# Strassen's products for most input projections of the second layer of a four-layer model on one core

## The chip, the core and the metric

The kernel runs on one core of a Trainium2 chip. The time is what the device takes for one execution, in microseconds. The core's engines are TensorE (PE, the matmuls; PEld is its loading of weights), VectorE (DVE), ScalarE (ACT), GpSimd (POOL) and SyncE (SP, which here only issues transfers). Each runs its own instructions in the order in which they stand in its queue, and waits on semaphores for the others.

## What is computed

A sequence of 1024 tokens with 16 learned ones ahead, 1040 in all, 1024 features each, passes through four residual layers: sliding-window attention, a gated linear recurrence (mLSTM), another one (HGRN2), and attention again. All of it is float32. The change is in the second layer:

```python
def mlstm_branch(u, w_in, conv_w, conv_b, gate_bias, h_gain, w_out, valid):
    q, k, v, ig, fg, og, z = _split(u @ w_in, B_SIZES)   # 1024, 1024, 2048, 8, 8, 2048, 2048
    qk = jax.nn.silu(causal_conv(jnp.concatenate([q, k], axis=-1), conv_w, conv_b))
    ...
    h = mlstm_chunkwise(qh, kh, vh, log_i, log_f)        # 8 heads, 128 keys, 256 values, blocks of 128
    h = jax.nn.sigmoid(og).reshape(...) * h
    h = rmsnorm(h, h_gain.reshape(B_HEADS, B_DV)).reshape(bsz, lp, B_W)
    return (h * jax.nn.silu(z)).astype(u.dtype) @ w_out

# for each layer i
u = rmsnorm(h, norm_gain[i])
h = h + branch(u, ...)
```

## The kernel before

Features lie on the partitions. `x` is the residual, one tile of 128 x 8 x 1040; `uh` and `ul` hold the normed tokens. A float32 factor is split into a high part of a shorter format (fp32r, which PE takes at full pace) and a low part, the rest: `split` is a cast on ACT (L212) and a subtraction on DVE (L213). A product of two float32 matrices is then three matmuls, high by high, high by low and low by high (`uh,wh`, `ul,wh`, `uh,wl` in the profile).

Tokens go in three chunks of 400, 384 and 256. `proj` (L253 for its matmuls) makes one tile of 128 output features: for each chunk 8 contraction tiles of 128 by 3 products, 24 matmuls that add up in one PSUM bank, and then `evac`, which takes the bank's content on: for a query or key the causal convolution (L1031 to 1045), for `og` a sigmoid times h (L1204), for `z` a silu times h (L546, L547). `sigmoid_from` (L525 to 529) makes the sigmoid. `weights` loads a tile of weights in two halves (L229, on SP) into one of two raw buffers and splits them into one of three buffers each for `wh` and `wl`. Values are made by `proj_vt`, and the output projection by `proj_out`: L397 for its matmuls, L400 for the addition to `x`.

The second layer has eight heads. `mixer(h)` is the recurrence of one head, with small matmuls and a chain through ACT and DVE (L1086 to L1179); `weave` mixes its steps with the projections of q for head h+1, k for h+2 and v for h+1. Then follow `og` (two tiles), `z` (two tiles), with three `stat` steps between (the norm of h, L1223), and then the output projection of this head, `oc[h]`. So q, k, v are made in the mixer's stage, and a head's h is done with after its own output projection; those of heads 6 and 7 are handed to the next layer's start.

The order on PE is the order in which the steps stand in one list, written out by hand; `later` puts a step some time behind the start of a list. Weights are asked for ahead, when the steps between add up to 12 us (`LOOKAHEAD`). Instructions of the other engines, SP's transfers among them, are put in order by a scheduler when the program is built. PSUM has 8 banks.

## Time and profile before

| | us |
|---|---|
| median of 3 runs | 2565.74 (2564.76 to 2566.45) |
| the profiled execution | 2567.49 |
| its span | 2565.7, so 1.8 lie around it |
| PE busy | 2523.8 |
| DVE busy | 2025.6 |
| ACT busy | 1750.1 |
| POOL busy | 245.8 |
| moved by DMA | 140.24 MB, 55 GB/s in the mean |

The granted clock of PE is 0.999 of full speed. A row of a view gives start and length of an instruction, its engine, its line in the kernel, the operation, and what it writes and reads by the program's names; "idle before" is the time its engine stood still just ahead of it, with what ended that. A row of a table by stage has, for a stretch from one time to another, the busy time of each engine with its number of instructions in brackets, the granted clock, the busy share of the DMA engines and the GB/s. Matmuls are pipelined, so a matmul's cost is read from the step between the starts of one and the next, not from its length.

### The profile page before, as it was taken

How to read it: one execution, taken by the hardware profiler on the slowest of the kernel's cores; microseconds unless marked ns; L12 is line 12 of the kernel's file. 1: busy time of each engine (PE TensorE's matmuls, PEld its weight loads, DVE VectorE, ACT ScalarE, POOL GpSimd, SP SyncE). 2: the span in 40 equal slices, each digit the busy share in tenths (PEclk: the TensorE clock that was granted, in tenths of full speed). 3: DMA queues.
4: the chain of work that ended last, by engine and by line, in shares of the span. 5: the costliest groups of instructions: out<-in, count | busy, mean ns of one | idle time of the engine just before them, and what ended most of it. 6: DMA issues, size and time to landing. Idle time of an engine off the chain costs nothing. (4 is left out here: it accounts for less than half of the span.)

```text
span 2565.7 us, 54823 instructions
## 1 busy us (share of the span) xinstructions
PE 2523.8 (98%) x20278; PEld 2471.9 (96%) x20278; DVE 2025.6 (79%) x5593; ACT 1750.1 (68%) x4719; POOL 245.8 (10%) x569
## 2 busy tenths in 40 slices
PE   9999999999999999999999999999999999999999
PEld 8899999999999999999999999999999999999999
DVE  7897898786767676767677788988878988987986
ACT  8766767576565656565675758877676857867772
POOL 0321221000000000000000001100010100321220
PEclk9999999999999999999999999999999999999999
DMA  5223112022232212121221111111111013212112
GB/s 159 62 58 96 58 55 69 27 56 51 50 51 50 46 50 51 46 51 49 48 52 55 54 44 34 35 35 35 43 34 42 28 52 94 65 49 77 56 38 83
DMA packets 103342, 140.24 MB, mean 55 GB/s; under 512 B 15369, under 2 KB 58514, under 8 KB 103074
## 3 DMA queue, kind: packets, MB, share of 16 engines
q1 hardware_dynamic: 102786, 136.20, 19.2%
q8 instruction: 160, 2.62, 0.4%
q14 instruction: 108, 0.88, 0.1%
q10 hardware_dynamic: 288, 0.52, 0.1%
HBM read 121.83 MB, written 4.27 MB: 49 GB/s over the span
## 5 line engine op out<-in xcount | busy, mean ns | idle before, releaser
L253 PE MATMUL pj<-uh,wh 128*128 128x384 f32 (+2 forms) x2688 | 901.7, 335 | 2.1 <-ACT uh L212 1.2
L253 PE MATMUL pj<-ul,wh 128*128 128x384 f32 (+2 forms) x2688 | 864.3, 322 | 1.0 <-DVE ul L473 0.5
L253 PE MATMUL pj<-uh,wl 128*128 128x384 f32 (+2 forms) x2688 | 863.7, 321 | 0.0
L253 PEld LDWEIGHTS pj<-uh,wh 128*128 128x128 f32 x2688 | 507.2, 189 | 10.6 <-issue 2.6
L253 PEld LDWEIGHTS pj<-ul,wh 128*128 128x128 f32 x2688 | 507.8, 189 | 5.6 <-DVE ul L213 1.4
L253 PEld LDWEIGHTS pj<-uh,wl 128*128 128x128 f32 x2688 | 506.8, 189 | 0.0
L213 DVE TENSOR_TENSOR wl<-wr,wh 128x512 fp32r<-128x512 f32 (+1 forms) x336 | 231.6, 701 | 70.7 <-ACT wh L212 68.2
L212 ACT CAST wh<-wr 128x512 fp32r<-128x512 f32 (+1 forms) x336 | 201.9, 613 | 92.0 <-PE pj L397 37.8
L397 PE MATMUL pj<-yh,wh 128*128 128x384 f32 (+2 forms) x768 | 252.7, 329 | 8.0 <-DVE x L400 5.3
L400 DVE TENSOR_TENSOR x<-x,pj 128x384 f32<-128x384 f32 (+2 forms) x480 | 234.2, 507 | 32.5 <-PE pj L397 31.3
L397 PE MATMUL pj<-yl,wh 128*128 128x384 f32 (+2 forms) x768 | 246.1, 320 | 1.3 <-DVE yl L213 1.3
L397 PE MATMUL pj<-yh,wl 128*128 128x384 f32 (+2 forms) x768 | 245.9, 320 | 0.0
L809 ACT ACTIVATE Sm<-Sm,s 128x257 f32<-128x257 f32 (+2 forms) x272 | 131.1, 483 | 91.5 <-DVE s L806 86.1
L812 POOL TENSOR_TENSOR Sm<-Sm,s 128x512 f32<-128x512 f32 (+2 forms) x136 | 137.0, 1007 | 401.4 <-DVE s L811 391.8
L529 ACT ACTIVATE t<-t 128x256 f32<-128x256 f32 (+2 forms) x240 | 118.2, 492 | 66.5 <-DVE t L528 65.7
L212 ACT CAST yh<-r 128x384 fp32r<-128x384 f32 (+2 forms) x120 | 57.0, 478 | 149.0 <-PE pj L397 131.3
L397 PEld LDWEIGHTS pj<-yh,wh 128*128 128x128 f32 x768 | 144.6, 188 | 11.7 <-DVE x L400 7.3
L397 PEld LDWEIGHTS pj<-yl,wh 128*128 128x128 f32 x768 | 144.7, 188 | 2.5 <-DVE yl L213 2.2
L358 PE MATMUL pj<-wh,uh 128*128 128x256 f32 (+1 forms) x504 | 145.8, 289 | 0.0
L397 PEld LDWEIGHTS pj<-yh,wl 128*128 128x128 f32 x768 | 144.3, 188 | 0.0
L358 PE MATMUL pj<-wl,uh 128*128 128x256 f32 (+1 forms) x504 | 142.0, 282 | 0.0
L358 PE MATMUL pj<-wh,ul 128*128 128x256 f32 (+1 forms) x504 | 141.7, 281 | 0.0
(345 smaller groups left out, 5784.0 us busy)
## 6 DMA issues: line engine op xcount, KB each, us to landing
wr<-in_b_win SPq DMA_DIRECT2D x124, 256.0 KB, 2.8
wr<-in_a_win SPq DMA_DIRECT2D x78, 256.0 KB, 2.7
wr<-in_c_win SPq DMA_DIRECT2D x64, 256.0 KB, 2.9
wr<-in_a_wout SPq DMA_DIRECT2D x32, 256.0 KB, 2.7
rw<-rowsd SPq DMA_DIRECT2D x64, 128.0 KB, 4.5
wr<-in_b_wout SPq DMA_DIRECT2D x32, 256.0 KB, 2.7
t<-t SPq DMA_DIRECT2D x100, 48.0 KB, 1.9
cs<-in_rope SPq DMA_DIRECT2D x11, 400.0 KB
```

Source lines behind the costliest of these rows:

```text
L212: s.copy(h, src)
L213: v.tensor_tensor(l, src, h.bitcast(F32), op=ALU.subtract)
L253: pe.matmul(acc[:, :cn], a[:, k, :], b[:, k, c0 : c0 + cn], start=(k == 0 and i == 0), stop=(k == KT - 1 and i == 2))
L358: pe.matmul(acc[:cn, :nc], a[:, k, c0 : c0 + cn], m[:, kk, :], start=(k == 0 and j == 0), stop=(k == KT - 1 and j == 2))
L397: pe.matmul(acc[:, :cn], a[:, k, mc], b, start=(k == 0 and i == 0), stop=(k == 1 and i == 2))
L400: v.tensor_tensor(x[:, m, c0 : c0 + cn], x[:, m, c0 : c0 + cn], acc[:, :cn], op=ALU.add)
L529: s.activation(a[:, :cn], a[:, :cn], AF.Exp)
L809: s.activation(Sm[:nq, u, : nk + 1], Sm[:nq, u, : nk + 1], AF.Exp, scale=-1.0, bias=st[:nq, u : u + 1], accum_out=den[:nq, u : u + 1])
L812: g.tensor_tensor(Sm[:nq, :, :nk], Sm[:nq, :, :nk], den[:nq].rearrange("p (u c) -> p u c", c=1).to_broadcast([nq, 2, nk]), op=ALU.mult)
```

## The change

Two 128-feature tiles of output are made together by a new function, `pair`: the first and the second key tile (`kk`), the query of head h with the key of head h+1 (`qk`, five of them, h from 2 to 6), both `og` tiles of a head (eight) and both `z` tiles of a head (seven, heads 0 to 6). These are 21 pairs. The other five tiles of that kind (q of heads 0, 1 and 7, k of head 0) and head 7's two `z` tiles stay with `proj`.

In a pair, the contraction's tiles 0 to 3, cut in two (0, 1 and 2, 3), the two output tiles, and the tokens 0 to 383 and 384 to 767 make a product of two by two blocks. It is computed with seven block products instead of eight (Winograd's form): `p1`, `p6`, `p5`, `p7` and the first parts of `c11`, `c12`, `c21`. The contraction's tiles 4 to 7 are added to the same banks in the usual way, and so is the whole of the last 272 tokens. The chunks of a pair are thus 384, 384 and 272 tokens.

What this takes besides:

- Sums of blocks of the normed tokens, once for the layer (`token_sums`): 16 additions or subtractions on POOL, 8 splits on ACT and DVE. They are kept in buffers that `x` had: `x` is now 24 tiles, leaves for DRAM in 24 transfers (`leave`) as its tiles are normed, and comes back in 24 (`back`) at the start of head 7's `z` tiles.
- Sums of blocks of the weights, for each pair: four additions or subtractions on POOL, and four splits, wholly on POOL (a cast and a subtraction each).
- For each pair one copy on ACT (`hold`) and eight additions on DVE (`add`) that put the products together; the result reaches `evac` in SBUF and not in PSUM. In a query's or key's pair the copy into the convolution's buffer falls away for two chunks of each tile.
- All output projections of heads 0 to 5 come at the end, since `x` is away until then. The rows of h of heads 0 to 5 go to DRAM (`park`) and come back (`fetch_y`).

Three places of the order. Names are the program's, with the number of the buffer behind some. First PE, where the mixer of head 0 ends and its `og` tiles are under way. Before, one contraction tile of `og` follows another (`pj` is the bank, `wh` and `wl` the weights):

```order
L253 MATMUL pj_8333<-ul,wh_8031 128x384
L253 MATMUL pj_8333<-uh,wl_8032 128x384
L253 MATMUL pj_8382<-uh,wh_8137 128x384
L253 MATMUL pj_8382<-ul,wh_8137 128x384
L253 MATMUL pj_8382<-uh,wl_8138 128x384
```

Now, behind the mixer's last output (`po`), `p6` in six matmuls, and then `p5` begins; `th` and `tl` are sums of tokens, high and low, `sh` and `sl` sums of weights:

```order
L1268 MATMUL po_8433<-Ch_8357,qwl_8336 128x258
L381 MATMUL pj_8446<-th_6970,sh_8182 128x384
L381 MATMUL pj_8446<-tl_6971,sh_8182 128x384
L381 MATMUL pj_8446<-th_6970,sl_8183 128x384
L381 MATMUL pj_8446<-th_7032,sh_8182 128x384
L381 MATMUL pj_8446<-tl_7033,sh_8182 128x384
L381 MATMUL pj_8446<-th_7032,sl_8183 128x384
L381 MATMUL pj_8454<-th_6966,sh_8177 128x384
```

A product takes two contraction tiles, six matmuls, and both operands can be sums. In all the list of PE has 126 rows fewer, six for each pair.

Second ACT, at the start of the layer, where it makes the high parts of the normed tokens (`uh`) of the second chunk and empties the banks of v (the COPY into `v`). Before:

```order
L212 CAST uh<-t_6535 128x384
L414 ACTIVATE v_6379<-v_6379 128x256
L273 COPY v_6632<-pj_6595 128x256
L967 COPY G_6474<-pj_6595 128x16
L212 CAST uh<-t_6548 128x384
L212 CAST uh<-t_6562 128x384
L212 CAST uh<-t_6609 128x256
```

Now four of the casts of token sums (`th<-ts`) stand between them:

```order
L225 CAST th_6966<-ts_6909 128x384
L1280 CAST Vh_7427<-v_6546 16x258
L225 CAST uh<-t_6568 128x384
L579 ACTIVATE v_6412<-pa_6646,consts 128x256
L225 CAST uh<-t_6573 128x384
L580 ACTIVATE v_6412<-v_6412 128x256
L225 CAST th_6970<-ts_6910 128x384
L225 CAST uh<-t_6587 128x384
L439 COPY v_6675<-pj_6636 128x256
L1139 COPY v_6507<-pj_6636 128x16
L225 CAST th_6974<-ts_6911 128x384
```

What stands behind a `th` cast waits on ACT until POOL has made that sum.

Third SP, at the end of the layer. Before, the weights of the output projection (`in_b_wout`) follow those of the last `z` tile (`in_b_win`) directly:

```order
L229 DMA wr_19291<-in_b_win 128x512
L229 DMA wr_19295<-in_b_win 128x512
L229 DMA wr_19421<-in_b_win 128x512
L229 DMA wr_19425<-in_b_win 128x512
L229 DMA wr_19545<-in_b_wout 128x512
L229 DMA wr_19549<-in_b_wout 128x512
```

Now 22 of the 24 transfers of x stand between the last half of the `z` weights and them, here the last five:

```order
L290 DMA x_18825<-away 128x256
L290 DMA x_18827<-away 128x256
L290 DMA x_18829<-away 128x256
L290 DMA x_18831<-away 128x256
L290 DMA x_18833<-away 128x256
L242 DMA wr_18932<-in_b_wout 128x512
L242 DMA wr_18936<-in_b_wout 128x512
```

The core of the diff:

```diff
+    away = dram.tile([KT, P, T], F32, name="away")
+
+    def leave(k, c0, cn):
+        sp.dma_start(away[k, :, c0 : c0 + cn], xt(k, c0, cn))
+
+    def back():
+        for n, (c0, cn) in enumerate(CHUNKS):
+            for k in range(KT):
+                sp.dma_start(new_x(n, k), away[k, :, c0 : c0 + cn])
+
+    def token_sums():
+
+        ts = [[None, None] for _ in range(4)]
+        held = {}
+
+        def sums(z):
+            def fn():
+                held[z] = t = [tpool.tile([P, 400], F32, tag=q, name=nm("ts"), bufs=YS)[:, :PW] for q in ("yh", "yl") * 2]
+
+                def add(i, k, c0):
+                    cs = slice(c0, c0 + PW)
+                    g.tensor_tensor(t[i], uh[:, k, cs].bitcast(F32), ul[:, k, cs].bitcast(F32), op=ALU.add)
+
+                add(0, z, 0)
+                add(2, z, PW)
+                g.tensor_tensor(t[0], t[2], t[0], op=ALU.subtract)
+                add(1, 2 + z, PW)
+                g.tensor_tensor(t[2], t[1], t[2], op=ALU.subtract)
+                g.tensor_tensor(t[1], t[1], t[0], op=ALU.subtract)
+                add(3, 2 + z, 0)
+                g.tensor_tensor(t[3], t[3], t[1], op=ALU.subtract)
+
+            return fn
+
+        def parts(z):
+            def fn():
+                for i, t in enumerate(held[z]):
+                    h = cpool.tile([P, 400], F32R, tag="x0", name=nm("th"), bufs=KT)[:, :PW]
+                    l = cpool.tile([P, 384], F32R, tag="x1", name=nm("tl"), bufs=KT)
+                    split(t, h, l)
+                    ts[i][z] = h, l
+
+            return fn
+
+        return [[0.0, fn(z), None] for z in range(2) for fn in (sums, parts)], ts
...
+    def pair(src0, src1, evac0, evac1, ts, scratch, follows):
+
+        st, acc = {}, {}
+        (a0, _), (b0, _), (c0, cn) = PAIRED
+
+        def pre():
+            ws = [tuple(wpool.tile([P, 1024], F32R, tag=z, name=nm(z), bufs=3) for z in ("wh", "wl")) for _ in range(2)]
+            raw = {}
+
+            def part(i, half):
+                z = slice(512 * half, 512 * half + 512)
+                raw[i] = raw_tile()
+                sp.dma_start(raw[i], (src0, src1)[i][:, z])
+                split(raw[i], *(w[:, z] for w in ws[i]))
+
+            part(0, 0)
+            part(1, 0)
+            a11, a12, a21, a22 = (raw[i][:, 256 * j : 256 * j + 256] for i in range(2) for j in range(2))
+            f, sums = scratch(), {}
+            f = [f[:, 256 * z : 256 * z + 256] for z in range(3)]
+
+            def parts(i, z):
+                sums[i] = h, l = [cpool.tile([P, 256], F32R, tag="x2", name=nm(q), bufs=KT) for q in ("sh", "sl")]
+                g.tensor_copy(h, z)
+                g.tensor_tensor(l, z, h.bitcast(F32), op=ALU.subtract)
+
+            g.tensor_tensor(f[0], a21, a22, op=ALU.add)
+            g.tensor_tensor(f[1], f[0], a11, op=ALU.subtract)
+            g.tensor_tensor(f[2], a11, a21, op=ALU.subtract)
+            parts(1, f[0])
+            g.tensor_tensor(f[0], a12, f[1], op=ALU.subtract)
+            for i, z in ((2, f[1]), (3, f[2]), (4, f[0])):
+                parts(i, z)
+            part(0, 1)
+            part(1, 1)
+            st["w"] = [tuple(z.rearrange("p (k c) -> p k c", c=P) for z in w) for w in ws]
...
+        def products(key, ops, n=PW, first=False, done=None, last=False):
+            def fn():
+                if first:
+                    acc[key] = psj()
+                for z, (a, b) in enumerate(ops()):
+                    for i, (p, q) in enumerate(((a[0], b[0]), (a[0], b[1]), (a[1], b[0]))):
+                        pe.matmul(acc[key][:, :n], p, q, start=(first and z == 0 and i == 0),
+                                  stop=(last and z == 1 and i == 2))
+                if done:
+                    done()
+
+            return [6 * n * MM, fn, None]
...
+        def add(dst, x0, key):
+            hi(lambda: v.tensor_tensor(dst, x0, bank(key), op=ALU.add))()
+
+        def hold():
+            st["t"] = t = tmp()[:, :PW]
+            hi(lambda: s.copy(t, bank("p1")))()
+
+        def put(*keys, place=False):
+            def f(dst=None):
+                if dst is None:
+                    dst = st["t"] if place else tmp()[:, :PW]
+                z = st["t"]
+                for key in keys:
+                    add(dst, z, key)
+                    z = dst
+                return dst
+
+            return f
...
+        two = range(2)
+        p1 = [products("p1", lambda: [(w(0, z), u(z, a0)) for z in two], PW, True, hold, True)]
+        p6 = [products("p6", lambda: [(sm(2, z), ts[1][z]) for z in two], PW, True, lambda: add(st["t"], st["t"], "p6"), True)]
+        p5 = [products("p5", lambda: [(sm(1, z), ts[0][z]) for z in two], PW, True, None, True)]
+        p7 = [products("p7", lambda: [(sm(3, z), ts[2][z]) for z in two], PW, True, lambda: add(st["t"], st["t"], "p7"), True)]
+        c11 = [products("y", lambda: [(w(0, 2 + z), u(2 + z, a0)) for z in two], first=True)]
+        c11 += rest("y", 0, a0, lambda: evac0(put("y"), None, 0, a0, PW))
+        c12 = [products("v", lambda: [(sm(4, z), u(2 + z, b0)) for z in two], first=True)]
+        c12 += rest("v", 0, b0, lambda: evac0(put("p5", "v"), None, 1, b0, PW))
+        c21 = [products("x", lambda: [(w(1, 2 + z), ts[3][z]) for z in two], first=True)]
+        c21 += rest("x", 1, a0, lambda: evac1(put("x", place=not follows), None, 0, a0, PW))
+        c22 = rest("w", 1, b0, lambda: evac1(put("p5", "w"), None, 1, b0, PW), first=True)
+        m0 = rest("c0", 0, c0, lambda: evac0(None, acc["c0"], 2, c0, cn), cn, (0, 2, 4, 6), True)
+        m1 = rest("c1", 1, c0, lambda: evac1(None, acc["c1"], 2, c0, cn), cn, (0, 2, 4, 6), True)
+        if follows:
+            steps = p1 + c11 + p6 + p5 + c12 + m0 + p7 + c21 + c22 + m1
+        else:
+            steps = p1 + c11 + p6 + p5 + c12 + p7 + c22 + c21 + m0 + m1
+        steps[0][2] = pre
...
+                if self.after is not None:
+                    self.after(k, c0, cn)
...
-                s.copy(raw[:, 3 : 3 + cn], acc[:, :cn])
+                if put is None:
+                    s.copy(raw[:, 3 : 3 + cn], acc[:, :cn])
+                else:
+                    put(raw[:, 3 : 3 + cn])
+                    acc = raw[:, 3 : 3 + cn]
...
+        def og_evac(h, c):
+            def f(put, acc, n, c0, cn):
+                cs = slice(c0, c0 + cn)
+                hr = R["h", h, c]
+                z = put() if put else acc[:, :cn]
+                a = sigmoid_from(z, cn)
+                v.tensor_tensor(hr[:, cs], hr[:, cs], a[:, :cn], op=ALU.mult)
...
+        kk = pair(win[9], win[17], ke[1], ke[2], ts, scratch, True)[0]
+        qk = {h: pair(win[8 * h], win[8 * h + 9], qe[h], ke[h + 1], ts, scratch, True)[0] for h in range(2, 7)}
...
+        og = {h: pair(win[8 * h + 4], win[8 * h + 5], og_evac(h, 0), og_evac(h, 1), ts, scratch, False) for h in range(8)}
+        zg = {h: pair(win[8 * h + 6], win[8 * h + 7], z_evac(h, 0), z_evac(h, 1), ts, scratch, False)[0] for h in range(7)}
+        zg[7] = flat(flat([one_tile(win[62 + c], z_evac(7, c)) for c in range(2)]))
...
+        zg[7][:0] = [[0.0, back, None], fetch_y(0), fetch_y(1)]
+        body += finish(rest, gates(7))
+        for h in range(6):
+            seq = flat(outs(oc[h]))
+            if 1 <= h < 5:
+                later(seq, (FETCH_AT, fetch_y(h + 1)))
+            body += seq
```

More of the change, by code (lines that the diff above doesn't have):

```diff
@@ L168, in hybrid_kernel, with new_x, xt @@
     v.memset(one, 1.0)
-    x = cpool.tile([P, KT, T], F32, name="x")
+    xs = {}
+    def new_x(n, k):
+        xs[n, k] = z = cpool.tile([P, CHUNKS[n][1]], F32, tag=f"x{n}", name=nm("x"), bufs=KT)
+        return z
+    def xt(k, c0, cn):
+        n = [c0 < a + b for a, b in CHUNKS].index(True)
+        o = c0 - CHUNKS[n][0]
+        return xs[n, k][:, o : o + cn]
     uh = cpool.tile([P, KT, T], F32R, name="uh")
@@ new lines, in pair, with w, sm, u @@
+    def pair(src0, src1, evac0, evac1, ts, scratch, follows):
[28 more added lines that the diff above has]
+            st["w"] = [tuple(z.rearrange("p (k c) -> p k c", c=P) for z in w) for w in ws]
+            st["s"] = {i: tuple(z.rearrange("p (k c) -> p k c", c=P) for z in w) for i, w in sums.items()}
+        def w(i, k):
+            return tuple(z[:, k, :] for z in st["w"][i])
+        def sm(i, z):
+            return tuple(q[:, z, :] for q in st["s"][i])
+        def u(k, o, n=PW):
+            return uh[:, k, o : o + n], ul[:, k, o : o + n]
+        def products(key, ops, n=PW, first=False, done=None, last=False):
[9 more added lines that the diff above has]
+            return [6 * n * MM, fn, None]
+        def rest(key, i, o, done=None, n=PW, ks=(4, 6), first=False):
+            return [products(key, lambda k=k: [(w(i, k + z), u(k + z, o, n)) for z in range(2)], n,
+                             first and k == ks[0], done if k == ks[-1] else None, k == ks[-1]) for k in ks]
+        def bank(key):
+            return acc[key][:, :PW]
+        def add(dst, x0, key):
[32 more added lines that the diff above has]
+        steps[0][2] = pre
+        return steps, dict(zip(range(3), (c21[-1], c22[-1], m1[-1])))
@@ L1234, in layer_b @@
-        qg = {h: conv_proj(win[8 * h], h, 1.0, ("q", h)) for h in range(8)}
-        kg = {h: conv_proj(win[8 * h + 1], 8 + h, 128 ** -0.5, ("k", h)) for h in range(8)}
+        def og_evac(h, c):
[3 more added lines that the diff above has]
+                z = put() if put else acc[:, :cn]
+                a = sigmoid_from(z, cn)
+                v.tensor_tensor(hr[:, cs], hr[:, cs], a[:, :cn], op=ALU.mult)
+                if ("sq", n) not in R:
+                    R["sq", n] = q = tpool.tile([P, 400], F32, tag="yl", name=nm("sq"), bufs=YS)[:, :cn]
+                    s.activation(q, hr[:, cs], AF.Square)
+                else:
+                    s.activation(a[:, :cn], hr[:, cs], AF.Square)
+                    v.tensor_tensor(a[:, :cn], a[:, :cn], R.pop(("sq", n)), op=ALU.add)
+                    R["sqs", n] = qs = [tpool.tile([P, 400], F32R, tag=z, name=nm(z), bufs=YS)[:, :cn]
+                                        for z in ("yh", "yl")]
+                    split(a[:, :cn], *qs)
+            return f
@@ new lines, in h_stat, with fn @@
+        def h_stat(h, n):
+            c0, cn = PAIRED[n]
+            def fn():
+                cs = slice(c0, c0 + cn)
+                q = tmp()[:, :cn]
+                sm = psa()
+                for i, z in enumerate(R.pop(("sqs", n))):
+                    pe.matmul(sm[:, :cn], R["ones"], z, start=(i == 0), stop=(i == 1))
+                rstd_from(sm, q, cn, 256)
+                for c in range(2):
+                    hr = R["h", h, c]
+                    v.scalar_tensor_tensor(hr[:, cs], hr[:, cs], R["hgain"][:, 2 * h + c : 2 * h + c + 1], q,
+                                           op0=ALU.mult, op1=ALU.mult)
+            return [2 * cn * MM, fn, None]
@@ new lines, in z_evac, with f, park, fn @@
+        def z_evac(h, c):
+            def f(put, acc, n, c0, cn):
+                z = put() if put else acc[:, :cn]
+                silu_into(lambda: R["h", h, c], z, slice(c0, c0 + cn), cn)
+            return f
+        parked = dram.tile([12, P, T], F32, name="parked")
+        def park(h):
+            def fn():
+                for c in range(2):
+                    sp.dma_start(parked[2 * h + c], R["h", h, c])
+            return [0.0, fn, None]
+        def fetch_y(h):
+            def pre():
+                for c in range(2):
+                    R["h", h, c] = row()
+                    sp.dma_start(R["h", h, c], parked[2 * h + c])
+            return [0.0, lambda: None, pre]
@@ L1236, in layer_b @@
+        t_steps, ts = token_sums()
+        qe = {h: conv_evac(h, 1.0, ("q", h)) for h in range(8)}
+        ke = {h: conv_evac(8 + h, 128 ** -0.5, ("k", h)) for h in range(8)}
+        qg = {h: one_tile(win[8 * h], qe[h]) for h in (0, 1, 7)}
+        kg = {0: one_tile(win[1], ke[0])}
+        kk = pair(win[9], win[17], ke[1], ke[2], ts, scratch, True)[0]
+        qk = {h: pair(win[8 * h], win[8 * h + 9], qe[h], ke[h + 1], ts, scratch, True)[0] for h in range(2, 7)}
         gsrc = [ins["b_wv0"][j][:, 272 * a : 272 * b] for a, b in ((0, 3), (3, 6), (6, 8))]
```

129 lines of the change are left out of this document (56 added, 73 removed).

## The prediction

> **What bounds the kernel now.** I read the page's busy times and chain first, then tables by stage for the second layer (about 478 to 1485 us), its waits, and single rows of TensorE, of VectorE and of GpSimd.
>
> ```profile
> span 2565.7 us, 54823 instructions
> PE 2523.8 (98%) x20278; PEld 2471.9 (96%) x20278; DVE 2025.6 (79%) x5593; ACT 1750.1 (68%) x4719; POOL 245.8 (10%) x569
> PE 11%; DVE 2%; ACT 1%; issue 0%; DMA 0%; POOL 0%; DVEq 0%; ACTq 0%
> ```
>
> PE is busy for 98% of the span, and the chain that can be followed to the end is nearly all PE. Stage by stage:
>
> ```profile
> core 0: us, PE busy (x) PEld busy (x) DVE busy (x) ACT busy (x) POOL busy (x), PEclk, DMA share, GB/s
> 10.00:20.00 10.00, 10.00 (x49) 9.97 (x49) 9.02 (x17) 8.72 (x19) 0.00 (x0) 1.00 0.91 293
> 440.00:460.00 20.00, 20.00 (x120) 19.71 (x120) 18.01 (x37) 8.30 (x17) 0.00 (x0) 1.00 0.03 9
> 478.00:500.00 22.00, 22.00 (x173) 21.08 (x172) 20.59 (x53) 16.20 (x46) 0.54 (x4) 1.00 0.08 26
> 500.00:510.00 10.00, 10.00 (x76) 9.69 (x76) 1.32 (x3) 4.20 (x12) 0.00 (x0) 1.00 0.15 52
> 547.00:597.00 50.00, 47.48 (x323) 45.80 (x323) 45.06 (x141) 42.55 (x124) 0.40 (x4) 1.00 0.19 41
> 547.00:657.00 110.00, 105.25 (x703) 102.41 (x703) 79.28 (x223) 81.33 (x218) 1.92 (x14) 1.00 0.22 49
> 657.00:1485.00 828.00, 827.94 (x5580) 824.76 (x5578) 575.54 (x1583) 522.52 (x1372) 11.73 (x85) 1.00 0.22 51
> 800.00:850.00 50.00, 50.00 (x340) 49.75 (x339) 40.97 (x125) 32.22 (x89) 0.30 (x3) 1.00 0.32 53
> 810.00:869.00 59.00, 59.00 (x428) 58.78 (x427) 43.32 (x146) 41.42 (x123) 1.17 (x10) 1.00 0.35 52
> 868.80:916.80 48.00, 48.00 (x306) 47.93 (x305) 28.57 (x59) 33.58 (x75) 0.69 (x4) 1.00 0.20 58
> 916.90:940.00 23.10, 23.10 (x149) 22.93 (x148) 17.05 (x38) 5.54 (x12) 0.00 (x0) 1.00 0.09 30
> ```
>
> From 657 to 1485 us PE has no gap (827.94 of 828), at granted clock 1.00: a matmul taken away there is time taken off, as long as the others keep up. One head lasts 130 us in three stages: a mixer with projections woven in (810 to 869), og and z (868.8 to 916.8), an output projection (916.9 to 940). Only around the first mixer does PE lose time: 4.75 us of 547 to 657. Its three longest waits there:
>
> ```profile
> engine line waited for: us in total, times, longest us
> PE pt L1177 <- ACT hn L1152: 1.3, 1, 1.3
> PE po L1086 <- ACT r L1037: 0.7, 1, 0.7
> PE pa L1223 <- ACT yh L212: 0.7, 1, 0.7
> ```
>
> **Step 1, matmuls removed.** The first matmul of each chunk of a z projection, then the first one of the next stage; 24 lie between one row and the next.
>
> ```profile
> start us, us, engine line op out<-in xcount [idle before <-releaser]
> 905.45 0.34 PE L253 MATMUL pj<-uh,wh 128*128 128x400 f32 x1
> 909.86 0.34 PE L253 MATMUL pj<-uh,wh 128*128 128x384 f32 x1
> 914.09 0.28 PE L253 MATMUL pj<-uh,wh 128*128 128x256 f32 x1
> 916.93 0.35 PE L397 MATMUL pj<-yh,wh 128*128 128x400 f32 x1
> ```
>
> So the step is 4.41/24 = 184 ns at 400 columns, 176 at 384, 118 at 256. It follows the columns, so fewer columns mean less time; 272 columns are then 118 × 272/256 = 126 ns. Two classical tiles cost 48 × (184 + 176 + 118) = 22.9 us. A pair costs 90 × 176 for the products and the classical half, and 48 × 126 for the last 272 tokens: 21.9 us. It saves 1.07 us, and 21 pairs 22.5 us (the order has 126 matmuls fewer; 126 × 176 ns is 22.2). This term is the surest. The moved output projections keep their matmuls.
>
> **Step 2, VectorE and GpSimd work added.** Per pair: eight adds of 128x384 on DVE out of PSUM, one ACT copy, and on POOL eight additions or subtractions and four casts of 128x256. In the queries' and keys' pairs ACT saves four copies.
>
> ```profile
> L400 DVE TENSOR_TENSOR x<-x,pj 128x384 f32<-128x384 f32 x8 | 4.2, 550 | 1.7 <-PE pj L397 1.7
> L812 POOL TENSOR_TENSOR Sm<-Sm,s 128x512 f32<-128x512 f32 x112 | 123.0, 1098 | 257.5 <-DVE s L811 247.9 <-DVE rq L674 5.1 <-PE pa L669 4.0
> L812 POOL TENSOR_TENSOR Sm<-Sm,s 128x288 f32<-128x288 f32 x16 | 11.3, 708 | 130.6 <-DVE s L811 130.5
> L213 DVE TENSOR_TENSOR wl<-wr,wh 128x512 fp32r<-128x512 f32 x10 | 6.7, 690 | 5.5 <-ACT wh L212 5.4
> ```
>
> An add is like L400, 0.55 us, but neighbours overlap (the last table row: 38 instructions, 24 of them such adds, in 17.05 us busy); I take 0.5, so 4 us a pair. DVE goes in the mixer stage from 43.3 to 47.3 of 57.9 us (82%), in og and z, two pairs, from 28.6 to 36.6 of 45.8 (80%). At 82% (800 to 850) PE lost nothing. POOL: 708 ns at 288 columns and 1098 at 512 give 0.65 us at 256, so 5.2 us a pair, and four casts of at most as much; by itself it fits.
>
> But the two engines hold each other up. The next rows are one GpSimd and one VectorE instruction of the first layer:
>
> ```profile
> 161.57 1.14 POOL L812 TENSOR_TENSOR Sm<-Sm,s 128x512 f32<-128x512 f32 x1 [6.97 <-DVE s L811]
> 161.73 1.53 DVE L213 TENSOR_TENSOR wl<-wr,wh 128x512 fp32r<-128x512 f32 x1
> ```
>
> The subtraction begins 0.16 us into POOL's and takes 1.53 us where its like take 0.69: 0.84 us lost of the 0.98 that POOL had left. Most DVE work of these stages (splits, products of gates and norms) reads two SBUF tiles, and now the gates of a pair do too, since their sum lies in SBUF. If each of POOL's eight catches one DVE instruction midway, DVE loses 8 × 0.65/2 = 2.6 us a pair (bounds 0 and 5.2): mixer stage 86%, og and z 91%.
>
> The Trainium skill, page "SBUF — State Buffer", section "Who interferes with whom", states this as a rule: a DVE instruction with two SBUF inputs contends with a GpSimd instruction that reads SBUF, one with a single SBUF input does not. The pair of rows above agrees (0.84 us). By the rule taken strictly each such meeting costs up to the whole 0.65 us, which is the upper bound, 5.2 us a pair; it speaks against putting the sums on GpSimd, and its outcome is rival two.
>
> What does a loaded DVE cost PE? At 90% (547 to 597) PE lost 2.5 us of 50, at 82% none: a line through both gives 0.31 us per point and 50 us. Yet at 90% (440 to 460) and at 94% (478 to 500) PE lost nothing; and the waits of the first mixer are on ACT's chain, not on DVE. I take an estimate of 0.6 us a head, 4.2 over the 21 pairs, seven heads of three (bounds 0 and 28, the line's value, worked out below). The second halves of a pair's weights wait, on SP, until POOL has read the first; behind them stand the mixer's row loads. The chain of loads, casts and sums needs about 10 us and can start a pair earlier, over 20 us, so I put nothing more on it.
>
> **Step 3, the start of the layer.** Sixteen POOL instructions on 128x384 (0.88 us by the two L812 rows, 14 us), eight ACT casts that wait for them, eight DVE subtractions. They fall into 478 to 500, where DVE is 94% busy, and ACT's casts stand ahead of casts of the normed tokens and of copies that empty PSUM. Cover: 8.7 us of idle DVE in 500 to 510, and PE's own queue. Bounds 0 and 8 (one half of the sums, 7 us, on the path, and one hold); I take 2.5, near the lower since DVE has that room directly behind. Fifteen transfers of x to DRAM go ahead of v's third weights on SP; a pair of issues takes 0.82 us there. Here the SPq row is that of these weights, and the VectorE row the last addition into x that the fifteen wait for:
>
> ```profile
> 473.90 0.54 DVE L400 TENSOR_TENSOR x<-x,pj 128x384 f32<-128x384 f32 x1
> 475.07 0.82 SPq L229 DMA_DIRECT2D wr<-in_b_wv  x2
> ```
>
> Fourteen can go as their tiles get ready before 474; the last, ready at 474.4, leaves 0.6 us to the weights' turn, so these are late by a few tenths, within the 2.5. **First mixer:** the kk pair comes into 547 to 606 with 4 + 2.6 us of DVE work, where DVE is at 90% already. Bounds 0 and 6.6; I take 3.
>
> **Step 4, the end of the layer.** All 24 tiles of x, 1040 × 1024 × 4 = 4.26 MB, come back ahead of the first output projection's weights. At the 293 GB/s of 10 to 20 us that is 14.5 us, and 24 issues take 10 us. The last use of a slot that x gets back is the last product of the eighth og pair; behind it come 48 matmuls of 126 ns (6 us) and z's two classical tiles (22.9): 29 us. Left are 14 us for weights (2.8 us to land) and casts.
>
> ```profile
> wr<-in_b_win SPq DMA_DIRECT2D x124, 256.0 KB, 2.8
> ```
>
> I take 0.5 (bounds 0 and 6); without cover it would be 14.5. The output projections in a row load DVE as each did alone (17.05 of 23.1), at no cost to PE; parked rows have 100 us and more to come back.
>
> **Sum**, against the profiled execution of 2567.49 us (span 2565.7, 1.8 around it): −22.5 + 4.2 + 2.5 + 3 + 0.5 = −12.3, so 2555.2. The runs' median is 1.75 us below the profiled one: 2553.4, rounded to 2553.
>
> **Rivals.**
>
> One, the saving arrives whole: DVE's added work lies in idle time, the lock costs no PE time. For it: no PE gap in 828 us, and PE unbroken at 94% DVE. Against it: the first mixer already stalls. 2565.7 − 22.5 = 2543 to 2546.
>
> Two, the lock makes DVE late. From 2.6 us a pair the line above takes over: mixer stage four points, 1.4 us; og and z nine points, 2.6 us; 4 us a head, 28 in all, and with the other terms −22.5 + 28 + 6 = +11.5: 2577, slower. It beats the saving from a PE loss of 2.4 us a head (22.5 − 6 over seven). For it: the rows at 161 us and 547 to 597. Against it: 440 to 500.
>
> Three, in-order queues: ACT held by the token sums, or x back late, at their upper bounds: 8 + 6.6 + 6 + 4.2 = 25 against 22.5, about 2568, no change. For it: ACT's order at the layer's start. Against: the 14 us left at the end.
>
> Four, the products don't shorten PE because narrower or more scattered matmuls step as slowly as 400 columns: 2566 or above. The rows of step 1 exclude most of it.
>
> **Chances.** My forecast (2546 to 2560) 0.55; rival one 0.14; two 0.17; three 0.12; four 0.02. The own range of the forecast is 2546 to 2560. For 8 in 10 I go down to 2543, into rival one, and up to 2568, which takes in rival three and leaves out most of rival two. About 0.2% (5 us) is what a measurement here can tell from no change: faster 0.70 (the first two), same 0.17 (most of three, some of two), slower 0.13 (most of two).
>
> **What would show it.** Step 1: rows of L381 at 176 ns steps, and og with z about 2.1 us shorter than 48. Step 2: POOL rows L352 to L358 near 0.65 us; DVE subtractions lengthened beside them, DVE at 86% and 91%; PE waits on DVE lines under 1 us a head. Step 3: PE gaps of 2 to 3 us between 478 and 547. Step 4: the first matmul of the output projections right behind z's last. I am wrong if PE waits for over 2 us a head (rival two), if L381 steps well off 176 ns, or if a gap over 5 us stands ahead of the output projections.

## The result

The changed kernel takes 2602.12 us (median of 4 runs, 2600.02 to 2605.43), the kernel before 2566.09 (4 runs, 2564.76 to 2569.42). The ratio is 1.0142 (95% interval 1.0129 to 1.0154): 36 us slower, where 13 us faster had been forecast. The profiled execution has a span of 2598.2 us.

### The profile page after: what moved, and what is told of

Same layout as the page of the kernel before. It is cut to its first block, busy times and chain, and to the rows that moved or that the text cites. A ratio compares the mean times of both kernels' runs of the same rounds, so it can differ in the third digit from the quotient of the medians.

```text
span 2598.2 us, 55392 instructions
## 1 busy us (share of the span) xinstructions
PE 2520.7 (97%) x20152; PEld 2455.8 (95%) x20152; DVE 2165.2 (83%) x5769; ACT 1768.4 (68%) x4724; POOL 450.7 (17%) x837
## 4 chain that ended last, share of the span: by engine, by line
PE 49%; DVE 26%; ACT 14%; DMA 4%; issue 4%; POOL 1%; SPq 0%; DVEq 0%; ACTq 0%; POOLq 0%
PE pj L266 16%; PE pj L563 14%; PE pj L381 4%; PE pj L524 4%; DVE wl L226 2%; DVE t L701 2%; DVE r L1218 2%; ACT t L700 2%; ACT t L699 2%; ACT wh L225 1%; PE po L1016 1%; PE pj L466 1%; PE pt L998 1%; ACT t L698 1%; DVE q L1218 1%
## 5 line engine op out<-in xcount | busy, mean ns | idle before, releaser
L266 PE MATMUL pj<-uh,wh 128*128 128x384 f32 (+2 forms) x1680 | 570.5, 340 | 3.7 <-ACT wh L225 1.7
L266 PE MATMUL pj<-ul,wh 128*128 128x384 f32 (+2 forms) x1680 | 540.3, 322 | 1.6 <-DVE ul L641 1.1
L266 PE MATMUL pj<-uh,wl 128*128 128x384 f32 (+2 forms) x1680 | 539.9, 321 | 0.3 <-DVE wl L226 0.2
L266 PEld LDWEIGHTS pj<-uh,wh 128*128 128x128 f32 x1680 | 317.5, 189 | 12.5 <-issue 2.6
L266 PEld LDWEIGHTS pj<-ul,wh 128*128 128x128 f32 x1680 | 317.8, 189 | 6.2 <-DVE ul L641 1.7
L266 PEld LDWEIGHTS pj<-uh,wl 128*128 128x128 f32 x1680 | 317.1, 189 | 0.9 <-DVE wl L226 0.9
L381 PE MATMUL pj<-uh,wh 128*128 128x384 f32 (+1 forms) x756 | 245.3, 325 | 0.5 <-DVE C L1348 0.5
L381 PE MATMUL pj<-uh,wl 128*128 128x384 f32 (+1 forms) x756 | 239.5, 317 | 0.0
L381 PE MATMUL pj<-ul,wh 128*128 128x384 f32 (+1 forms) x756 | 239.4, 317 | 0.0
L702 ACT ACTIVATE t<-t 128x384 f32<-128x384 f32 (+3 forms) x240 | 118.0, 492 | 63.2 <-DVE t L701 61.9
```

The costliest lines, as they stand in the source:

```text
L266: pe.matmul(acc[:, :cn], a[:, k, :], b[:, k, c0 : c0 + cn], start=(k == 0 and i == 0), stop=(k == KT - 1 and i == 2))
L381: pe.matmul(acc[key][:, :n], p, q, start=(first and z == 0 and i == 0), stop=(last and z == 1 and i == 2))
L702: s.activation(a[:, :cn], a[:, :cn], AF.Exp)
```

## The profile after

From the page of the changed kernel: the span, the engines, the chain of waits.

```profile
span 2598.2 us, 55392 instructions
PE 2520.7 (97%) x20152; PEld 2455.8 (95%) x20152; DVE 2165.2 (83%) x5769; ACT 1768.4 (68%) x4724; POOL 450.7 (17%) x837
PE 49%; DVE 26%; ACT 14%; DMA 4%; issue 4%; POOL 1%; SPq 0%; DVEq 0%; ACTq 0%; POOLq 0%
```

The chain now passes through DVE for 26% and ACT for 14% of the span, where it was 2% and 1%. PE's busy time is 3 us less than before, although 22.5 us of matmuls are gone. By stage (the layer's start, the two stretches behind it, one head from its mixer's first matmul to the next head's, and the output projections at the end):

```profile
core 0: us, PE busy (x) PEld busy (x) DVE busy (x) ACT busy (x) POOL busy (x), PEclk, DMA share, GB/s
478.00:500.00 22.00, 17.89 (x121) 16.06 (x120) 21.79 (x38) 13.77 (x38) 11.31 (x15) 0.85 0.19 60
500.00:547.00 47.00, 45.48 (x311) 44.35 (x310) 35.76 (x64) 27.02 (x67) 16.05 (x20) 1.00 0.17 48
547.00:657.00 110.00, 94.16 (x607) 91.08 (x607) 83.97 (x227) 73.22 (x195) 20.75 (x41) 0.94 0.19 48
789.70:898.80 109.10, 105.79 (x714) 103.37 (x713) 90.49 (x230) 76.72 (x198) 28.50 (x50) 1.00 0.21 59
1320.00:1480.00 160.00, 160.00 (x1025) 159.74 (x1024) 122.69 (x273) 73.99 (x163) 2.49 (x7) 1.00 0.34 106
```

At the start PE has 17.89 of 22 us where it had 22.00; a later head has gaps of 3.3 us where it had none. At the end, 1320 to 1480, there is no gap: x comes back in time.

The layer can be cut at the first matmul of each mixer. Times in us between these matmuls; the second column has the before with its five moved output projections (22.85 us each) set where they now stand, the third also without the 1.07 us a pair that the products save.

| from, to | before, outputs moved | with the saving | after | lost |
|---|---|---|---|---|
| layer's first matmul, mixer 0 | 64.7 | 64.7 | 75.2 | 10.5 |
| mixer 0, mixer 1 (3 pairs) | 114.3 | 111.1 | 127.8 | 16.7 |
| mixer 1, mixer 5 (12 pairs) | 427.6 | 414.8 | 437.4 | 22.6 |
| mixer 5, a fixed matmul of the third layer (6 pairs) | 496.1 | 489.7 | 499.9 | 10.2 |

What PE waits for: from 478 to 552, then the five longest of 552 to 680, then from 679 to 1117, four heads. After what is waited for stand the us in total, the number of waits and the longest.

```profile
PE pj L524 <- DVE ul L226: 4.1, 3, 1.9
PE pj L266 <- ACT wh L225: 1.4, 1, 1.4
...
PE pa L1404 <- ACT yh L225: 4.1, 2, 3.9
PE po L1268 <- ACT Wh L225: 3.6, 1, 3.6
PE pj L381 <- DVE kwh L1310: 2.5, 1, 2.5
PE pt L1359 <- ACT hn L1334: 1.4, 1, 1.4
PE pm L1285 <- DVE r L1224: 1.3, 1, 1.3
...
PE pt L479 <- ACT t L450: 5.4, 4, 1.3
PE pa L1404 <- ACT yh L225: 3.8, 10, 0.6
PE pa L1404 <- DVE yl L226: 3.7, 6, 0.9
PE po L1268 <- ACT qwh L225: 0.6, 3, 0.2
```

No wait names GpSimd. PE waits for what DVE and ACT make: the normed tokens (`ul`) at the start, and in each head the norm's matmuls (L1404) and the transposes of the values (L479). What DVE does at the start, beside GpSimd, from the timeline:

```profile
start us, us, engine line op out<-in xcount [idle before <-releaser]
488.12 2.30 POOL L303 TENSOR_TENSOR ts<-uh,ul 128x384 f32<-128x384 f32 x2 [0.39 <-DVE ul L226]
490.38 1.31 POOL L309 TENSOR_TENSOR ts<-ts,ts 128x384 f32<-128x384 f32 x1
491.77 1.19 POOL L310 TENSOR_TENSOR ts<-ts,ts 128x384 f32<-128x384 f32 x1
...
488.15 1.39 DVE L610 SCALAR_TENSOR_TENSOR t<-x,ngain,t 128x384 f32<-128x384 f32 x1
489.46 1.37 DVE L226 TENSOR_TENSOR ul<-t,uh 128x384 fp32r<-128x384 f32 x1
490.75 1.35 DVE L610 SCALAR_TENSOR_TENSOR t<-x,ngain,t 128x384 f32<-128x384 f32 x1
492.03 1.35 DVE L226 TENSOR_TENSOR ul<-t,uh 128x384 fp32r<-128x384 f32 x1
```

The two engines take turns: each DVE subtraction takes 1.36 us, and GpSimd's instructions 1.2 to 1.3. An undisturbed `ul` of this size took 0.55 us in the kernel before. In the heads the lengthening is seen in the groups (instructions of 789.7 to 898.8; the last row is of 680 to 790); where GpSimd makes no sums (`e13` below) the first two take 609 and 612 ns in a head:

```profile
L1218 DVE SCALAR_TENSOR_TENSOR r<-t,bcols,r 128x384 f32<-128x384 f32 x6 | 4.8, 803 | 0.0
L1408 DVE SCALAR_TENSOR_TENSOR r<-r,bcols,t 128x384 f32<-128x384 f32 x4 | 3.5, 889 | 0.0
L352 POOL TENSOR_TENSOR sl<-f,sh 128x256 fp32r<-128x256 f32 x12 | 9.8, 820 | 0.9
```

## The experiments

Theory A: GpSimd's sums hold DVE up, and the chains through DVE and ACT come late for PE. Later expectations call it A1, with A2 (the products wait for GpSimd's results) and F (the raw buffers that it holds) beside it. Against it stood B (steps stand too early for the longer chain of a pair). C, D, E and G are about the surroundings of the products: C, the transfers of x and of rows or the late output projections cost time; D, the output projection between two heads had given the other engines time to catch up; E, the chunks or the new places of steps cost it; G, asking for two tiles' weights at once does.

### Which part of the change costs what

The sums of the weights left out (`e1`): in `pre` the additions and `parts` fall away.

```diff
-            return tuple(q[:, z, :] for q in st["s"][i])
+            return w(i % 2, z)
```

> Leaves out the sums of the weights and their splits on GpSimd (12 instructions a pair, 21 pairs); the products take plain weights in their place, so PE's list, the adds and the token sums stay. In the changed kernel the heads lose about 6 us of PE time each and the first head 17, some 43 us in all from the first mixer on. Theory A (GpSimd's instructions lengthen VectorE's, about 6 us a head, and the late sums and gates make PE wait): most of that comes back, about 2565 us (2560 to 2572), and VectorE instructions lengthened in the heads fall from about 9 us a head to the 2.5 of before. Theory B (the steps that wait, above all the norm of h, stand too early for the longer chain of a pair, with or without GpSimd): 2590 or above, with the same waits at the norm's matmuls.

Measured 2568.25 us (ratio to before 1.0006, 0.9995 to 1.0017). That is in the range of theory A; of the 60 us lost, 34 hang on these 252 GpSimd instructions. A head (773.2 to 877.6) takes 104.4 us.

The sums of the tokens left out (`e2`):

```diff
-        return [[0.0, fn(z), None] for z in range(2) for fn in (sums, parts)], ts
+        return [], [[(uh[:, z, :PW], ul[:, z, :PW]) for z in range(2)] for _ in range(4)]
```

> Leaves out the sums of the tokens (16 GpSimd instructions, 8 ACT casts, 8 VectorE subtractions at the layer's start); the products take plain tokens. The changed kernel loses 10.5 us from the layer's first matmul to the first mixer. Theory A (there GpSimd and VectorE take turns, each instruction of VectorE 0.55 becoming 1.36 us): that loss goes, about 2591 us (2587 to 2595). If the loss comes from x leaving for memory ahead of the values' weights instead: unchanged, about 2602.

Measured 2594.68 us (2591.55 to 2597.8). From the layer's first matmul to mixer 0 it takes 65.5 us, against 75.2 with the sums and 64.7 before: the start's loss is theirs. Of these 9.7 us, 7.4 reach the end. That x leaves for memory, which this run keeps, costs the start under 1 us.

The products undone, all else kept (`e4`); `rest` runs over all eight contraction tiles, no sums, no adds:

```diff
-        c11 = [products("y", lambda: [(w(0, 2 + z), u(2 + z, a0)) for z in two], first=True)]
-        c11 += rest("y", 0, a0, lambda: evac0(put("y"), None, 0, a0, PW))
+        c11 = rest("y", 0, a0, lambda: evac0(None, acc["y"], 0, a0, PW), PW, full, True)
...
```

> Undoes the products alone: each pair is made with eight block products and emptied out of PSUM, without sums, splits of sums and adds; the chunks of 384, 384 and 272, x leaving and returning, the parked rows and the output projections at the end stay. Theories A and B alike: that surrounding costs nothing, so the time of the kernel before, 2566 us (2562 to 2570). Theory C (transfers of x and rows, or the late output projections, cost it): 2580 or above.

Measured 2580.36 us (2578.18 to 2583.91; ratio 1.0060, 1.0037 to 1.0083). The surroundings are not free: 14 us. C holds in part. From 680 to 1200 us its longest wait is this one, up to 1.8 us at a time:

```profile
PE pt L455 <- ACT t L426: 7.6, 5, 1.8
```

### Is it GpSimd's reading?

GpSimd only writes (`e6`): memsets instead of the sums and of their splits.

```diff
-                g.tensor_copy(h, z)
-                g.tensor_tensor(l, z, h.bitcast(F32), op=ALU.subtract)
+                g.memset(h.bitcast(F32), 0.0)
+                g.memset(l.bitcast(F32), 0.0)
+                g.memset(l.bitcast(F32), 0.0)
```

> GpSimd's instructions for the weight sums only write now: two memsets in the place of each addition or subtraction, one in the place of each cast. They stand at the same places, PE waits for them as before and the order on PE stays; left out are the sums. e1, without these instructions, took 2568. Theory A1 (GpSimd's reads lengthen VectorE's two-input instructions): as without them, 2568 (2563 to 2574), VectorE lengthened by about 2.5 us a head. Theory A2 (the products wait for GpSimd's results, or GpSimd's mere presence in the queues): 2590 or above.

Measured 2567.75 us (ratio 1.0005, 0.9994 to 1.0017): as without them. One head:

```profile
776.30:880.60 104.30, 104.21 (x713) 103.29 (x713) 83.18 (x231) 76.96 (x197) 12.34 (x50) 1.00 0.23 62
```

In its groups, that of the convolution, which had 803 ns above, and one of the memsets:

```profile
L1220 DVE SCALAR_TENSOR_TENSOR r<-t,bcols,r 128x384 f32<-128x384 f32 x6 | 3.7, 610 | 0.0
L351 POOL MEMSET sh<- 128x256 f32 x12 | 3.8, 313 | 56.6 <-PE pj L383 56.0
```

With as many GpSimd instructions in a head (x50 in both, 36 of them memsets for the splits), DVE is busy for 83.18 us and not 90.49, with one instruction more: 7.3 us a head, 2.4 a pair, was lengthening. With none of these instructions (`e1`) DVE's time in a head is much the same, 83.52 us, so the memsets lengthen nothing:

```profile
773.20:877.60 104.40, 104.32 (x713) 103.36 (x713) 83.52 (x231) 76.88 (x197) 1.85 (x14) 1.00 0.22 62
```

This edit changes more than the reading. The 168 memsets that stand for the additions wait for nothing and all ran at the layer's start (482.7 to 547.3 us), and the memsets are shorter than what they replace (GpSimd busy 12.34 us, not 28.50), so the chain of sums is shorter too. But PE waits for GpSimd in neither kernel. How much a reading instruction's length adds to the harm is not shown apart.

Other numbers read (`e7`), so that no raw buffer of weights is held:

```diff
-            a11, a12, a21, a22 = (raw[i][:, 256 * j : 256 * j + 256] for i in range(2) for j in range(2))
+            a11, a12, a21, a22 = (uh[:, 2 * i + j, 400:656].bitcast(F32) for i in range(2) for j in range(2))
```

> The same additions, subtractions and casts on GpSimd, but read from the normed tokens instead of the raw weights, so no raw buffer is held until GpSimd has read it, and the second halves of the weights may load at once; left out: the sums are of other numbers. Theory A1 (GpSimd's reads themselves): 2602 (2596 to 2608). Theory F (the raw buffers that it holds make weights late): near 2568 to 2585.

Measured 2598.98 us (2597.34 to 2600.62): 3 us under the changed kernel. So what GpSimd reads hardly matters, and the held buffers account for about 3 us of the 34 (two runs here).

The weight sums on DVE and ACT (`e8`), nothing left out: `g.tensor_tensor` becomes `v.tensor_tensor`, `g.tensor_copy` becomes `s.copy`.

> The whole computation, with the sums of the weights on VectorE (8 instructions of 128x256, about 0.42 us each, 3.4 us a pair) and their casts on ACT, nothing of them on GpSimd. Theory A1 with room on VectorE (the 2.1 us a pair lost to GpSimd were the harm, and 3.4 us of plain work are about as much): 2590 to 2604, no gain over the changed kernel, since VectorE is filled either way. If it is only the meeting of the two engines and not VectorE's fill: near e1, 2568 to 2578.

Measured 2584.22 us (2583.03 to 2585.4), 18 us under the changed kernel and below what A was held to give. The expectation that DVE's fill decides was wrong: here DVE is busy for 90.63 of 105.6 us in a head (785.2 to 890.8), as long as in the changed kernel in 109.1, and PE loses 0.9 us (104.72 of 105.6 busy) and not 3.3:

```profile
785.20:890.80 105.60, 104.72 (x713) 103.34 (x713) 90.63 (x255) 79.84 (x209) 1.87 (x14) 1.00 0.21 61
```

So the same busy time of DVE costs PE less when it is DVE's own work than when it is lengthening.

### Or the place of the norm's steps?

The norm 14 us behind its chunk and not 7 (`e3`, `STAT_LAG`):

> The whole kernel as changed, but the norm's steps stand 14 us and not 7 us behind the chunk that they wait for. Theory A (VectorE has no room, whoever waits): the waits move elsewhere, 2597 to 2604 us. Theory B (only the place of these steps): 3.4 us for each of about six heads and the 4 us of the first come back, about 2580 (2575 to 2585), with no waits at the norm's matmuls.

Measured 2606.73 us (2604.74 to 2608.71), a little above the range of A and far above that of B. The norm's matmuls wait no more, and this wait has come in their place (680 to 1200), at the first block of the next mixer:

```profile
PE po L1323 <- DVE Wh L1296: 14.5, 5, 6.1
```

At 9 us, with head 5's steps 2 us later (`e14`):

> The changed kernel (2602) with one thing moved: the norm's steps 9 us behind their chunk and not 7, and head 5's two us later, as e13 (2549) has them. e13 gained 19 us over e10 by that. If the place of the norm's steps is worth as much with GpSimd at work: about 2583. Theory A1 (with GpSimd's reads VectorE has no room, so waits only move, as they did at 14 us in e3): 2595 to 2606.

Measured 2604.77 us (2604.62 to 2604.93). With GpSimd's sums in it, the place of the norm gives nothing back. B falls as a cause of its own.

### The surroundings

Outputs between the heads, x at home, classical products (`e5`):

```diff
+                    if h < 5:
+                        body += flat(outs(oc[h]))
```

> As e4 (classical products in the chunks of 384, 384 and 272), and besides x stays in its buffers, no row is parked, and the output projections of heads 0 to 5 stand again between the heads. e4 took 2580, 14 us over the kernel before, and waits 2 us a head where the transposed values wait for an ACT copy. Theory D (the output projection between two heads was the time in which ACT and VectorE worked off the gates; without it the next mixer starts with a backlog): 2566 (2563 to 2569), transposes without a wait. Theory E (the chunks of 384, 384 and 272 themselves, or the new places of steps): stays at 2576 or above.

Measured 2601.30 us (2599.87 to 2602.73): 21 us more than e4, not less. D falls, and E's time (2576 or above) is met. The same with the two tiles' weights asked for one after the other (`e9`):

```diff
-        steps[0][2] = pre
+        steps[0][2] = pre(0)
+        (c21 if follows else c22)[0][2] = pre(1)
```

> As e5 (classical products, chunks of 384, 384 and 272, x at home, output projections between the heads), but the two tiles of a pair ask for their weights one after the other, each ahead of its own first step, and not both together ahead of the pair. e5 took 2601. Theory G (both tiles' loads and splits come in one burst and occupy two of the three weight buffers early, so ACT's and VectorE's other work is late and the transposes wait): 2566 to 2572. If the chunks or the places of the steps are the cause: above 2590.

Measured 2594.68 us (2591.63 to 2597.73). The transposes wait no more, so asking for both weights at once was their trouble here; 28 us remain. They are found in the kernel before with nothing but the chunks changed (`e11`: `proj(..., PAIRED)` in q, k, og, z and the norm):

> The kernel before with one thing changed: the second layer's q, k, og and z projections, and the norm of h, go in chunks of 384, 384 and 272 tokens in place of 400, 384 and 256; order, weights and all else as before. If the chunks cost what e4 and e5 lost: 2576 or above. If not: 2566 (2563 to 2569).

Measured 2601.32 us (2600.68 to 2601.95; ratio 1.0131). Its four longest waits from 470 to 1620:

```profile
PE po L1087 <- ACT Ch L213: 6.6, 5, 1.4
PE pj L398 <- ACT yh L213: 6.4, 5, 1.3
PE po L1087 <- DVE Cl L214: 5.3, 5, 1.1
PE pt L1178 <- ACT hn L1153: 2.7, 1, 2.7
```

L398 is the output projection. It still takes 400 tokens first, and their last 16 now lie in z's second chunk; that this is why it waits for its splits (`yh`) is read from the code, not tried. So the chunks of 384, 384 and 272 are a cost of 35 us where the outputs stand between the heads; with the outputs at the end (e4) these waits are not there, and the time is 21 us shorter than in e5. So moving the outputs seems to have helped the change, by taking that mismatch out of the heads.

e4 with the weights asked for apart (`e12`, the same diff as e9):

> As e4 (classical products, 2580; x away, rows parked, output projections at the end), but the two tiles of a pair ask for their weights one after the other, as in e9. In e9 the waits of the transposes for the ACT copy (7.6 us in e4 from 680 to 1200) were gone. Theory G (e4's 14 us come from asking for two tiles' weights at once): 2566 to 2571, and no waits of the transposes. If the journey of x, the parked rows or the late output projections carry a part: 2573 or above.

Measured 2575.90 us (2570.43 to 2576.56; ratio 1.0032, 1.0017 to 1.0047). So 4.5 of the 14 us are the joint loading. There are three runs on each side, and they spread over 6 us, but the traces agree: the four heads of the table below take 429.9 us here and 434.4 in e4. The other 9.5 lie in small waits, none over 2.7 us in sum, and with no place of their own; what makes them is left open.

### Versions that should pay

Nothing on GpSimd (`e10`): as e8, the token sums on DVE too, and the keys of heads 1 and 2 classical, 20 pairs.

```diff
-        kg = {0: one_tile(win[1], ke[0])}
-        kk = pair(win[9], win[17], ke[1], ke[2], ts, scratch, True)[0]
+        kg = {h: one_tile(win[8 * h + 1], ke[h]) for h in range(3)}
+        kk = flat(kg[1]) + flat(kg[2])
```

> The change with three things moved: the sums of the weights on VectorE and ACT as in e8 (2584), the sums of the tokens on VectorE too, and the first two key tiles of heads 1 and 2 made classically, so 20 pairs are left and GpSimd does nothing of it. e8 gained 1.3 us a head from the second head on against the kernel before, and lost 9 us at the layer's start and 12 in the first head, where VectorE has no room. Theory A1: the start returns to within 3 us of before, the first head to within 4; about 2562 (2556 to 2570), at or a little under the kernel before. If VectorE's fill at the start is the limit whoever makes the sums: 2575 or above.

Measured 2567.95 us (10 runs, 2564.44 to 2571.07; ratio 1.0006, 0.9996 to 1.0016): the time of the kernel before, in A's range. The start takes 67.3 us, the first head 114.4. What still waits from 680 to 1200:

```profile
PE pa L1404 <- ACT yh L225: 4.4, 6, 2.7
PE pa L1404 <- DVE yl L226: 2.1, 7, 0.4
```

Now the norm 2 us later (`e13`):

```diff
-STAT_LAG, PARK_LAG, T_STEP, FETCH_AT = 7000.0, 6000.0, 1500.0, 10000.0
+STAT_LAG, PARK_LAG, T_STEP, FETCH_AT = 9000.0, 6000.0, 1500.0, 10000.0
...
-                    for n, lag in ((1, 7000.0), (2, 4000.0), (0, 3000.0)):
+                    for n, lag in ((1, 9000.0), (2, 6000.0), (0, 5000.0)):
```

> As e10 (nothing on GpSimd, 20 pairs, 2568, the same as before), with the norm's steps 9 us behind the chunk they wait for and not 7, and those of head 5 two us later. e10's waits at the norm's matmuls are about 1 us a head and 3 us once. If they can be had back: 2560 (2556 to 2565), under the kernel before. If the wait moves to the next mixer's first block, as in e3: 2566 to 2572.

Measured 2549.26 us (5 runs, 2547.66 to 2550.98; ratio to before 0.9936, 0.9922 to 0.9949): faster than both kernels, by 17 and 53 us, and well below the 2556 to 2565 that had been expected: 19 us came back, where e10's waits at the norm were taken to be worth 8. One head:

```profile
761.30:865.10 103.80, 103.80 (x713) 103.38 (x713) 90.21 (x256) 79.04 (x211) 1.87 (x14) 1.00 0.23 63
```

All that PE waits for in the four heads from 656.5 to 1072.3:

```profile
PE pa L1341 <- DVE kwh L1310: 0.6, 1, 0.6
```

Last, in this kernel the weight sums go back to GpSimd and nothing else is changed (`e15`, e8's diff turned round):

> e13 (2549) with the sums of the weights put back on GpSimd, 20 pairs; the token sums stay on VectorE. Theory A1: GpSimd's reads cost the heads what they cost e6 against the changed kernel, 34 us for 21 pairs, so about 2580 (2572 to 2588). If the norm's place was the cause all along: 2549 to 2556.

Measured 2585.61 us (2584.33 to 2586.89): 36 us more than e13. Four heads, 663.6 to 1103.4, the longest waits:

```profile
PE pt L479 <- ACT t L450: 5.4, 4, 1.3
PE po L1323 <- DVE Wh L1296: 4.3, 4, 1.1
PE po L1268 <- ACT qwh L225: 2.3, 4, 0.6
PE pa L1341 <- DVE kwh L1310: 1.6, 4, 0.4
```

Where PE's time went, stage by stage, in the kernels that tell it (stages as in the first table, us):

| stage | before, outputs moved | after | e1 | e4 | e8 | e13 | e15 |
|---|---|---|---|---|---|---|---|
| start | 64.7 | 75.2 | 73.9 | 64.7 | 73.9 | 67.6 | 67.5 |
| first head | 114.3 | 127.8 | 118.7 | 112.9 | 126.6 | 109.9 | 117.8 |
| four heads | 427.6 | 437.4 | 417.0 | 434.4 | 422.5 | 415.8 | 439.8 |
| rest | 496.1 | 499.9 | 494.0 | 503.2 | 495.8 | 492.0 | 497.9 |

## Why the prediction was wrong

**Step 1 was right.** Matmuls of L381 step by 175 ns at 384 columns and 125 at 272 (medians), 176 and 126 had been taken. Without GpSimd's sums the four heads take 415.8 us (e13), within 1 us of 427.6 less 12 pairs at 1.07. Rival four is out.

**Step 2 named the mechanism and sized the lengthening rightly, and went wrong in the next sentence.** I had 2.6 us a pair for what DVE loses beside GpSimd; it is 2.4 (90.49 against 83.18 us a head, three pairs). The eight adds of a pair, put at 4 us, take 4.4 (24 of them 13.1 us in a head). The step that failed is "What does a loaded DVE cost PE?": I took 0.6 us a head, 4.2 in all; the runs show 34 (e1), 34 (e6) and 36 (e15). PE stands still for 3.3 us a head, over the 2 us that I had named as the sign of being wrong. Rival two, which I gave 0.17, had the place and the mechanism. By its 4 us a head the four heads would have lost 16 us, and the first 7 with the 3 of step 3; they lost 22.6 and 16.7.

The way of pricing it was wrong on both sides. I read PE's loss from DVE's share of busy time, low because 440 to 460 and 478 to 500 had PE unbroken at 90 and 94%. But e13 has DVE at 87% of a head (90.21 of 103.8) and PE without a gap, and the changed kernel has it at 83% with 3.3 us of gaps. The share does not tell. DVE's busy time in a head is the same, 90 us, once made of instructions with their own length, and once of fewer that are stretched beside GpSimd: single ones of 0.55 to 0.61 us take up to 1.1 in the heads and 1.4 at the start, inside chains (gate, norm, split) that PE awaits at a fixed place. Why chains of unstretched work fit and these don't is argued from that, not tried.

The Trainium skill, page "SBUF — State Buffer", section "Who interferes with whom", states that a DVE instruction with two SBUF inputs contends with a GpSimd instruction that reads SBUF, and not with one that only writes it. The traces agree on both halves: 1.36 us for 0.55 beside reads at the start, 610 ns for 803 when GpSimd only writes. The prediction quoted the first half as speaking against the change; what it said of a single input holds on that page only outside DVE's two-port modes. By the rule the harm was to be expected; I kept it for a rival.

**Step 3 was sized wrongly.** I took 2.5 us for the start, bounds 0 and 8; it lost 10.5, of which 9.7 go with the token sums (e2). I had counted 14 us for GpSimd's sixteen sums; they took 20.1, in the groups of 470 to 552 (the eight of L303 alone 10.5). The upper bound had half of the sums and 1 us more in it; beside them one DVE instruction after another takes 1.36 us for 0.55. The cover in 500 to 510 lay behind the waits: 4.1 of PE's 5.5 us of waits fall before 500. The waits are not all: at a granted clock of 0.85 the 22 us from 478 to 500 lose up to another 3.3 by estimate (0.15 × 22), which the prediction had nowhere. For the first mixer I took 3 us; the first head lost 16.7, and the weight sums alone account for 9 of it (127.8 against 118.7 in e1). In e10 and e13, where DVE makes the sums, the start is 67.3 and 67.6 us; that this is my 2.5 is luck, since I had the sums on GpSimd.

**Step 4 was right, and what I had not listed was not.** x comes back unseen and the end has no gap. But the surroundings of the products (e4) cost 14 us that no term had: I had put nothing on the joint loading of two tiles' weights (about 4.5 us by e12), and not asked what new chunks do to what waits for them. Yet e13 has all of them and saves 17.1 of 20 × 1.07 = 21.4 us. So they are not a fixed price. That they come from the order in which the other engines' work falls is argued, not tried.

**The rivals.** One (the whole saving) and four are out; three (in-order queues) is seen in part at the start, where ACT stood 4.0 us at the casts of token sums until GpSimd had made them, though what PE waited for there is mostly DVE's `ul` (4.1 of 5.5 us). Two is what happened in the heads, and the total is 2602, not its 2577, because the start, the first head and the surroundings lost more as well.

## What to carry to other kernels

Work that is put on an idle engine isn't free if it lengthens the instructions of a busy one: price it at what it does to them inside the chains that the bound engine awaits, and not by busy shares; and try first the same work on the busy engine itself, where it can be ordered. A change that regroups chunks touches every consumer that still cuts elsewhere. And here a step's place by hand was only worth tuning once the disturbance was gone: the same 2 us were worth nothing beside GpSimd (e14) and 19 us without it (e13 against e10).

## What the runs showed of the hardware

How much hangs on reading was not expected so clearly. 36 GpSimd instructions a head that only write, 313 ns each, leave DVE's busy time as it is without them (83.18 us in e6, 83.52 in e1); the same number that read, and take longer, add 7.3 us to it and cost 34 us over the layer.

Also unexpected: after one of its waits PE is slow for a while. In the changed kernel, a pause of 2.45 us and what follows:

```profile
559.03 0.34 PE L381 MATMUL pj<-th,sl 128*128 128x384 f32 x1
561.83 0.66 PE L381 MATMUL pj<-uh,sh 128*128 128x384 f32 x1 [2.45 <-DVE kwh L1310]
562.29 0.52 PE L381 MATMUL pj<-ul,sh 128*128 128x384 f32 x1
...
564.85 0.51 PE L381 MATMUL pj<-uh,wh 128*128 128x384 f32 x1
565.17 0.36 PE L381 MATMUL pj<-ul,wh 128*128 128x384 f32 x1
565.36 0.34 PE L381 MATMUL pj<-uh,wl 128*128 128x384 f32 x1
```

The table by stage, for this stretch (granted clock 0.60):

```profile
562.00:566.00 4.00, 4.00 (x15) 4.00 (x16) 4.00 (x10) 2.64 (x7) 0.00 (x0) 0.60 0.40 129
```

For 3.3 us (561.83 to 565.17) a matmul steps by 320 ns in place of 176, ten of them: 1.6 us more than the wait itself. The granted clock is 0.85 in the start's row and 0.94 in the first mixer's, against 1.00 before. The waits of up to 1.3 us in each head's transposes bring no such slow stretch: the granted clock of the head from 789.7 to 898.8 is 1.00. The Trainium skill, page "TensorE: Matmul & The Clock Gate", section "What's actually happening", has the clock at half after an idle window of about 3.4 us and full again after as long a busy one. The trace agrees on the length of the recovery (3.3 us) and on the half pace, not on the pause: 2.45 us were enough here.
